# Mixture-of-experts stage: gather from x, one weight buffer more, other load and store shapes

## The chip, the cores and the metric

The kernel runs on one core of one Trainium2 chip. The metric is the device time of one execution in microseconds (us), the median of the runs that were made; lower is better. The profile comes from one further execution of the same program.

## The reference

The model is a float32 transformer over 256 tokens of 1024 channels: a first block of two layers, then a second block whose last part is a mixture of experts. Only that last part is touched. 32 experts stand in 4 groups of 8; every token is sent to the best two experts of its best group. The weights of one expert are two 1024x512 matrices (gate, up) and one 512x1024 matrix (down), 6 MB together, so all experts are 192 MB that must be read from HBM once.

```python
def rmsnorm_2(x, g):
    xf = x.astype(jnp.float32)
    y = xf * lax.rsqrt(jnp.mean(xf * xf, axis=-1, keepdims=True) + EPS)
    return (y * g.astype(jnp.float32)).astype(x.dtype)

def hier_moe(h, w_rg, b_rg, w_re, b_re, w_gate, w_up, w_down):
    ...
    weights = p_grp * top_p / jnp.sum(top_p, axis=-1, keepdims=True)
    expert = grp * EXPERTS_PER_GROUP + top_i
    ...
    def run_block(args):
        e, tok, w = args
        xb = xt[tok]
        hid = jax.nn.silu(xb @ w_gate[e]) * (xb @ w_up[e])
        return (hid @ w_down[e]) * w[:, None].astype(xb.dtype)
    ...

def second_block(...):
    ...
        x = x + hier_moe(rmsnorm_2(x, g_moe[l]), w_router_group[l], ...)
    return rmsnorm_2(x, g_final)
```

## The kernel before, in words

The kernel is one long program over the stages of the model; the stage `moe` is its last. The 32 experts are worked on in 8 groups of four (`for p in range(8)`). Each of the four gets 32 token slots, so that the 128 slots of a group fill the 128 columns of a TensorE operand.

**Routing.** `xT = self.xtile("h", "rT")` holds x transposed. It lives in the tile that the pool `xpool` hands out under the tag "xTh"; the pool has one buffer per tag, so a later tile of that tag takes the same memory once every reader of the earlier one is done. 16 matmuls called `rt` read it, eight for each half of the tokens. VectorE (DVE) makes from them the choice of experts (`A`), the place of each token in its expert's slots (`rk`) and the mixing weights (`Wt`).

**Gather.** `xk` is x times the reciprocal root mean square `r` of each token, with its channels reordered. It is written by two ScalarE (ACT) instructions (L1378) into the tile "xTh". `oh` is a one-hot matrix of tokens by slots (L1390), and the matmuls `xg` multiply `xk` by it; DVE copies the result, times the norm's gain, to `xe`, the gathered tokens (L1401).

**Weights.** They come in loads of 1 MB (one expert's half of a matrix, 128 partitions by 2048 numbers, 8 KB in one run for each partition). All are issued on one queue, that of SyncE (SP), and each is issued only after the one before it was issued (`self.after(*self.queue)`), in the order gate, up, down, group by group. A load goes to the next buffer of a rotation, `wrot`, through `wtile`, and its issue waits until the readers of that buffer's earlier contents are done. SP works through its queue in order: while one issue waits, those behind it wait as well. Before each issue SP also waits for the load eight issues earlier, since the semaphores DMAHW0 to DMAHW7 are used in turn. Three gate loads are issued earlier, by `moe_loads`. The rotation begins with

```python
self.wrot = (self.early + self.trot[:1] + [b, lambda: self.xtile("l", "w"), b, b]
             + hb + mw[4:5] + hb + [mw[i] for i in (8, 7, 0, 3, 2, 1, 5, 6)])
self.nw = 2
```

`self.early` has three entries, the buffers of the early loads, so the first load of the stage itself takes entry 3, counted from 0. There are 21 entries. `b` and `hb` are buffers that the stages before this one used for weights too, `xtile("l", ...)` is the tile "xTl".

**A group.** The matmuls `gu` multiply `xe` by gate and up; DVE and ACT make silu(gate) times up; it is transposed (`hT`); the matmuls `y` multiply it by down; two matmuls `acc` for each half of the channels scatter the result, weighted, to the tokens (`ot`, made from `oh` times `Wt` in `scatter`).

**The last group.** Its last 4 MB of up and its 8 MB of down are loaded in 256 KB pieces, runs of 2 KB (`pieces(..., True)`, L1425). Down is taken by halves of the output channels: when half `h` is done, x is added (`xo`, in tile "xTh", L1505), and `final` makes the final norm: squares on ACT (L1748), a root on ACT (L1754), four small steps on DVE, the products (L1532, L1535, L1536), and four stores of 256 KB (L1538).

Of the kernel before, what the change touches and what calls it, by code (L numbers as in the profile page):

```python
# [8 lines left out]
F32 = mybir.dt.float32  # L9
# [3 lines left out]
AF = mybir.ActivationFunctionType  # L13
OP = mybir.AluOpType
# [3 lines left out]
P = 128  # L18
S = 256
D = 1024  # L20
# [24 lines left out]
class K:  # L45
# [1270 lines left out]
    def moe(self, x):  # L1316
        nc, a = self.nc, self.a
        V = nc.vector
# [10 lines left out]
        def w1(i):  # L1329
# [4 lines left out]
        mw = [w1(i) for i in range(9)]  # L1334
        mp = self.pool("moe", 1, ctx)
        hb = [lambda: self.hbpool.tile([P, 2048], F32, tag="wh", name="w")] * 2
        self.wrot = (self.early + self.trot[:1] + [b, lambda: self.xtile("l", "w"), b, b]
                     + hb + mw[4:5] + hb + [mw[i] for i in (8, 7, 0, 3, 2, 1, 5, 6)])
        self.nw = 2

# [32 lines left out]
        acc = self.accs(pctx)  # L1373


        xk = self.xtile("h", "xk").rearrange("p (t k n) -> p t k n", t=2, k=8)
        for t in range(2):
            nc.scalar.activation(xk[:, t], x[:, t].rearrange("s (p k) -> s k p", k=8), AF.Copy, scale=r[:, t:t + 1])  # L1378
        oh = {}

        def four(m):
            return m.rearrange("p t (i n) -> p t i n", i=4)

        def over(m, p):
            return m[:, :, 4 * p:4 * p + 4, None].to_broadcast([P, 2, 4, CAP])

        def gather(p):

            oh[p] = mp.tile([P, 2, P], F32, tag=f"oh{p % 2}", name="oh")
            V.tensor_tensor(four(oh[p]), io[:, None, None].to_broadcast([P, 2, 4, CAP]), over(rk, p), op=OP.is_equal)  # L1390
            xe = mp.tile([P, 8, P], F32, tag="xe", name="xe")
            yield xe
            n = 4 if p else 2
            for c in range(2):
                for k0 in range(4 * c, 4 * c + 4, n):
                    ps = self.ps("xg")[:, 0:n * P].rearrange("p (k n) -> p k n", k=n)
                    for i in range(n):
                        for t in range(2):
                            self.mm(ps[:, i], xk[:, t, k0 + i], oh[p][:, t], t == 0, t == 1)
                    ks = slice(k0, k0 + n)  # L1400
                    V.tensor_tensor(xe[:, ks], ps, self.gcol8[:, ks, None].to_broadcast([P, n, P]), op=OP.mult)  # L1401
                yield

        def scatter(p):
# [7 lines left out]
            V.tensor_copy(ot, ps[:, 0:256].rearrange("p (t n) -> p t n", t=2))  # L1412
            return ot

        def pieces(src, fine):


            n1, n2 = src[0].shape[1:]
            if not fine:
                return [self.first.pop(0) if self.first else self.load(v) for v in src]  # L1420
            w = [self.wtile(n1, n2) for _ in src]
            for k in range(n1):
                for i in range(4):
                    with self.after(*self.queue):
                        self.queue = [nc.sync.dma_start(w[i][:, k], src[i][:, k]).ins]  # L1425
            return w

        def part(m, k, i):
            return m[:, k, CAP * i:CAP * i + CAP]
# [1 line left out]
        nxt = gather(0)  # L1431
        xe = next(nxt)
        next(nxt)
        Wt = next(routes)
        for p in range(8):
            last = p == 7
            y = self.gpool.tile([P, 2, 512], F32, tag="gain", name="y")
# [1 line left out]
            for w in (wg, wu):  # L1439
                ps = self.ps("gu")  # L1440
                for c in range(2):
                    ch = pieces([self.in_rows(w[4 * p + i], c) for i in range(4)], last and w is wu and c == 1)
                    for k in range(4):
                        for i in range(4):
                            self.mm(ps[CAP * i:CAP * i + CAP, :], part(xe, 4 * c + k, i), ch[i][:, k],
                                    c == 0 and k == 0, c == 1 and k == 3, tile_position=(0, CAP * i))
                    next(nxt, None)
                hs.append(ps)
# [1 line left out]
            s = y[:, 0]  # L1450
            nc.scalar.activation(s, hs[0], AF.Silu)  # L1451
            sk = y[:, 1].rearrange("s (k p) -> s k p", k=4)
            turn = "s (k p) -> s k p" if last else "s (p k) -> s k p"
            V.tensor_tensor(sk, s.rearrange(turn, k=4), hs[1].rearrange(turn, k=4), op=OP.mult)  # L1454
            ot = scatter(p)
            if not last:
                nxt = gather(p + 1)
                xe = next(nxt)
                next(nxt)
                next(nxt)  # L1460
            else:
                self.tc.keep_in_program_order(nc.scalar.preload_act_table_set("sqrt_and_others"))
                gf = self.final_gain()
                o = self.wtile(2, D)
                xo = self.xtile("h", "xo").rearrange("p (t n) -> p t n", t=2)
                fin = Norm(self, xo, None, None, (), pool=mp)
            ps = self.ps("hT")
            for f in range(4):
# [12 lines left out]
            def back(h):  # L1481
# [4 lines left out]
                for t in range(2):  # L1486
                    self.mm(acc[t][h], ot[:, t], y[:, h], p == 0, last)

            if not last:
                for c in range(2):  # L1490
                    ch = pieces([self.out_rows(wd[4 * p + i], c) for i in range(4)], False)
                    for k in range(2):
                        for h in range(2):
                            down(h, 2 * c + k, [v[:, :, h * 512:(h + 1) * 512] for v in ch], k)
                for h in range(2):
                    back(h)
            else:
                for h in range(2):
                    cs = slice(h * 512, (h + 1) * 512)
                    ch = pieces([wd[4 * p + i, :, cs].rearrange("(k p) n -> p k n", p=P) for i in range(4)], True)  # L1500
                    for k in range(4):
                        down(h, k, ch, k)
                    back(h)
                    for t in range(2):
                        V.tensor_tensor(xo[:, t, cs], x[:, t, cs], acc[t][h], op=OP.add)  # L1505
                        self.final(xo, gf, o, fin, t, h)
        pctx.close()
        self.spill(x, xo, nrm, r, rk, A, Wt, mp, gf, o)
        ctx.close()

    def final_gain(self):
# [9 lines left out]
            nc.scalar.activation(w[:, 0, cs], ps, AF.Copy)  # L1521
        return w[:, 0]

    def final(self, x, g, o, fin, t, c):

        nc = self.nc
        V = nc.vector
        xs, gs, os_ = [[v[:, t, k * 512:(k + 1) * 512] if v is not g else v[:, k * 512:(k + 1) * 512]
                        for k in range(2)] for v in (x, g, o)]
        fin.rms_part(t, c)  # L1530
        if c == 0:
            nc.gpsimd.tensor_tensor(os_[0], xs[0], gs[0], op=OP.mult)  # L1532
            return
        r = fin.r[:, t:t + 1]
        V.scalar_tensor_tensor(os_[1], xs[1], r, gs[1], op0=OP.mult, op1=OP.mult)  # L1535
        nc.scalar.activation(os_[0], os_[0], AF.Copy, scale=r)  # L1536
        for k in range(2):
            nc.sync.dma_start(self.out[0, t * P:(t + 1) * P, k * 512:(k + 1) * 512], os_[k])  # L1538

    def spill(self, x, xo, nrm, r, rk, A, Wt, mp, gf, o):  # L1540

# [12 lines left out]
        with tc.If(most > CAP):  # L1554
            with tc.tile_pool(name="spd", bufs=1, space=bass.MemoryType.DRAM) as dp:
# [47 lines left out]
                            V.scalar_tensor_tensor(xs, y, we[:, t], xs, op0=OP.mult, op1=OP.add)  # L1603
                fin = Norm(self, xo, None, None, (), pool=mp)
                for t in range(2):
                    for c in range(2):
                        self.final(xo, gf, o, fin, t, c)

    def lazy(self, f, *a):
        yield  # L1610
# [78 lines left out]
class Norm:  # L1689
# [49 lines left out]
    def rms_part(self, t, c):  # L1739
# [11 lines left out]
            V.tensor_scalar(ss, ss, EPS, None, op0=OP.add)  # L1751
            return

        nc.scalar.activation(u, y, AF.Sqrt, bias=ss)  # L1754
        V.tensor_scalar(v, y, ss, -0.5, op0=OP.add, op1=OP.mult)
        V.reciprocal(y, u)
        V.tensor_scalar(u, y, y, v, op0=OP.mult, op1=OP.mult)
# [400 lines left out]
```

## Time and profile before

| | |
|---|---|
| median of 3 runs | 1354.72 us (1354.0 to 1354.75) |
| the profiled execution's own time | 1352.86 us |
| its span (first to last event of the trace) | 1351.2 us |
| TensorE busy | 1238.8 us, 92% of the span |
| mean granted TensorE clock | 0.972 of full speed |
| loads from HBM | 343.38 MB |

The span is what the trace shows; 1.66 us of the profiled execution's time lie outside it. The median of the runs is 1.86 us above the profiled execution. A pair of figures such as 950.00:1300.00 is a stretch in us from the start of the span. The share of an engine is a mean over stages that differ: a stretch is read by its own rows.

### The profile page before, as it was taken

The page shows a single profiled execution, that of the slowest core. Times are in us where ns is not written, and L with a number is a line of the kernel's source. Part 1 is how long each engine was busy: PE and PEld are TensorE (multiplying, and loading weights), DVE is VectorE, ACT ScalarE, POOL GpSimd, SP SyncE. Part 2 cuts the span into 40 slices and gives each one's busy share as a digit, 9 for nine tenths or more (in the row PEclk, how much of TensorE's full clock was granted, in tenths as well). Part 3 has the DMA queues.
Part 4 walks back from the last instruction along what each step waited for, and adds up shares of the span by engine and source line. Part 5 has one row for each costly group of instructions (what it writes and reads, how often), then busy time and mean ns, then how long its engine had stood idle before and what let it go on. Part 6 is the DMA issues. An engine that isn't in the chain of part 4 may idle for free.

```text
span 1351.2 us, 20184 instructions
## 1 busy us (share of the span) xinstructions
PE 1238.8 (92%) x8427; PEld 917.3 (68%) x8427; DVE 647.6 (48%) x1137; ACT 485.3 (36%) x784; POOL 47.3 (4%) x72
## 2 busy tenths in 40 slices
PE   8899999999999999999999999999777778778886
PEld 7786899999998899999999998964122212222211
DVE  9955866666589766666776587431000001000001
ACT  3273644444577544444556565440000000000002
POOL 4010000000100000000300000000000000000000
PEclk9989999999999999999999999999999898999888
DMA  9401955544434765544562758789999999999996
GB/s 267 105 7 48 355 183 191 191 131 150 141 125 156 271 222 190 191 130 136 168 188 94 242 196 284 287 322 422 421 422 421 422 421 422 421 422 421 421 389 241
DMA packets 143436, 345.79 MB, mean 256 GB/s; under 512 B 9863, under 2 KB 100063, under 8 KB 120302
## 3 DMA queue, kind: packets, MB, share of 16 engines
q1 hardware_dynamic: 141418, 339.40, 68.2%
q0 software_dynamic: 1888, 5.06, 1.3%
q8 instruction: 67, 1.10, 0.3%
q14 instruction: 27, 0.22, 0.1%
q10 hardware_dynamic: 36, 0.01, 0.0%
HBM read 343.38 MB, written 1.06 MB: 255 GB/s over the span
## 4 chain that ended last, share of the span: by engine, by line
PE 62%; DMA 27%; DVE 7%; ACT 3%; issue 1%; SPq 0%; DVEq 0%; ACTq 0%
PE gu L77 21%; PE acc L77 15%; DMA w<-in_w_exp_down_dram 9%; DMA w<-in_w_exp_gate_dram 7%; DMA w<-in_w_exp_up_dram 7%; PE z L77 4%; PE qk L77 3%; PE y L77 3%; PE v L77 2%; PE mqk L77 2%; PE prj L77 2%; DMA b<-in_w_exp_gate_dram 1%; DMA b<-in_w_exp_up_dram 1%; PE psT L1711 1%; PE cq L77 1%
## 5 line engine op out<-in xcount | busy, mean ns | idle before, releaser
L182 DVE TENSOR_TENSOR wh<-w,wh 128x1024 fp32r<-128x1024 f32 x229 | 276.1, 1223 | 136.3 <-ACT wh L181 136.1
L181 ACT ACTIVATE wh<-w 128x1024 fp32r<-128x1024 f32 x229 | 236.7, 1055 | 194.4 <-PE gu L77 68.0
L77 PE MATMUL gu<-fxh,wh 128*128 128x256 f32 x1408 | 253.3, 281 | 0.7 <-ACT fxh L181 0.7
L77 PE MATMUL gu<-w,xe 128*32 128x512 f32 x920 | 178.6, 668 | 50.5 <-DMA w<-in_w_exp_gate_dram 28.0
L77 PEld LDWEIGHTS gu<-fxh,wh 128*128 128x128 f32 x1408 | 217.9, 190 | 1.7 <-ACT fxh L181 0.9
L77 PE MATMUL gu<-fxl,wh 128*128 128x256 f32 x704 | 197.8, 281 | 0.0
L77 PEld LDWEIGHTS gu<-w,xe 128*32 128x32 f32 x920 | 39.6, 120 | 168.1 <-issue 67.5
L77 PEld LDWEIGHTS gu<-fxl,wh 128*128 128x128 f32 x704 | 133.1, 189 | 0.8
L77 PE MATMUL y<-w,hT 128*32 128x512 f32 x456 | 103.1, 611 | 17.3 <-DMA w<-in_w_exp_down_dram 11.9
L77 PE MATMUL acc<-wh,hh 128*128 128x512 f32 x352 | 109.5, 393 | 0.0
L77 PEld LDWEIGHTS y<-w,hT 128*32 128x32 f32 x456 | 24.4, 110 | 88.5 <-DMA w<-in_w_exp_down_dram 42.1
L77 PEld LDWEIGHTS acc<-wh,hh 128*128 128x128 f32 x352 | 64.4, 188 | 12.3
L1412 DVE COPY ot<-owT 128x256 f32<-128x256 f32 x8 | 3.4, 425 | 138.4 <-PE owT L1410 138.4
L77 PE MATMUL acc<-wh,hl 128*128 128x512 f32 x176 | 68.6, 390 | 0.0
L1454 DVE TENSOR_TENSOR y<-y,gu 128x512 f32<-128x512 f32 x8 | 8.1, 1013 | 110.6 <-PE gu L77 100.8
L1451 ACT ACTIVATE y<-gu 128x512 f32<-128x512 f32 x8 | 4.8, 597 | 151.9 <-PE gu L77 151.9
L1485 DVE COPY y<-y 128x512 f32<-128x512 f32 x7 | 4.8, 692 | 105.9 <-PE y L77 105.9
L1471 ACT ACTIVATE hT<-hT 128x512 f32<-128x512 f32 x8 | 4.8, 597 | 137.5 <-PE hT L1469 137.5
L77 PE MATMUL qk<-oxh,wh 128*128 128x256 f32 x256 | 49.1, 287 | 0.0
L77 PE MATMUL z<-mxh,wh 128*128 128x256 f32 x256 | 47.7, 285 | 0.0
L1483 ACT ACTIVATE y<-y 128x512 f32<-128x512 f32 x9 | 5.4, 597 | 114.6 <-PE y L77 114.6
L77 PE MATMUL gu<-b,xe 128*32 128x512 f32 x104 | 37.8, 682 | 7.1 <-DMA b<-in_w_exp_gate_dram 4.2
(539 smaller groups left out, 2047.3 us busy)
## 6 DMA issues: line engine op xcount, KB each, us to landing
w<-in_w_exp_gate_dram SPq DMA_DIRECT2D x57, 1024.0 KB, 19.8
w<-in_w_exp_up_dram SPq DMA_DIRECT2D x54, 1024.0 KB, 19.8
w<-in_w_exp_down_dram SPq DMA_DIRECT2D x51, 1024.0 KB, 19.8
w<-in_ffn_w_gate_dram SPq DMA_DIRECT2D x22, 1024.0 KB, 5.7
w<-in_ffn_w_up_dram SPq DMA_DIRECT2D x22, 1024.0 KB, 6.8
w<-in_ffn_w_down_dram SPq DMA_DIRECT2D x22, 1024.0 KB, 5.1
w<-in_w_in_dram SPq DMA_DIRECT2D x20, 1024.0 KB, 5.9
w<-in_odd_w_in_dram SPq DMA_DIRECT2D x12, 1024.0 KB, 7.3
```

The lines of the kernel that those rows point to most:

```text
L77: self.lastmm = self.nc.tensor.matmul(out, lhsT, rhs, start=start, stop=stop, **kw).ins
L181: return (self.nc.scalar.activation(h, src, AF.Copy).ins, (eng or self.nc.vector).tensor_tensor(l, src, h.bitcast(F32), op=OP.subtract).ins)
L182: (eng or self.nc.vector).tensor_tensor(l, src, h.bitcast(F32), op=OP.subtract).ins)
L1412: V.tensor_copy(ot, ps[:, 0:256].rearrange("p (t n) -> p t n", t=2))
L1451: nc.scalar.activation(s, hs[0], AF.Silu)
L1454: V.tensor_tensor(sk, s.rearrange(turn, k=4), hs[1].rearrange(turn, k=4), op=OP.mult)
L1471: nc.scalar.activation(hT, ps.rearrange("p (f n) -> p f n", f=4), AF.Copy)
L1483: nc.scalar.activation(y[:, h], yps[h], AF.Copy)
L1485: V.tensor_copy(y[:, h], yps[h])
L1711: k.turned = k.nc.tensor.transpose(ps[:, i * P:(i + 1) * P], xg[:, t, (4 * c + i) * P:(4 * c + i + 1) * P], k.ident).ins
```

## The change

Five things change, all in the last stage.

1. The gather's matmuls read x itself (a reordered view). `oh` is multiplied by `r` instead (a new DVE instruction for each group), and the mixing weights are divided by `r` once (`ri`, `Wr`), so that `oh` times `Wr` is what it was. The two ACT instructions that wrote `xk` are gone. The second half of the routing is put behind an `xe` copy.
2. The tile "xTh" becomes a 22nd entry of `wrot`, between the third `b` and `hb`, that is entry 8.
3. The last group's up, and the first half of its down, come in 1 MB loads with runs of 8 KB, as in the other groups. The other 4 MB of down come in four loads of 1 MB, each over the four experts, in runs of 2 KB.
4. `xo` takes a buffer of the rotation.
5. The final norm is split in two functions: the second half does both token tiles' roots before the ACT products, and there is one store of 512 KB for each token tile.

```diff
-        self.wrot = (self.early + self.trot[:1] + [b, lambda: self.xtile("l", "w"), b, b]
+        self.wrot = (self.early + self.trot[:1] + [b, lambda: self.xtile("l", "w"), b, b, lambda: self.xtile("h", "w")]
                      + hb + mw[4:5] + hb + [mw[i] for i in (8, 7, 0, 3, 2, 1, 5, 6)])
...
-        xk = self.xtile("h", "xk").rearrange("p (t k n) -> p t k n", t=2, k=8)
-        for t in range(2):
-            nc.scalar.activation(xk[:, t], x[:, t].rearrange("s (p k) -> s k p", k=8), AF.Copy, scale=r[:, t:t + 1])
+        xk = x.rearrange("s t (p k) -> s t k p", k=8)
...
             V.tensor_tensor(four(oh[p]), io[:, None, None].to_broadcast([P, 2, 4, CAP]), over(rk, p), op=OP.is_equal)
+            self.lastoh = V.tensor_tensor(oh[p], oh[p], r[:, :, None].to_broadcast([P, 2, P]), op=OP.mult).ins
...
-        Wt = next(routes)
+
+        ri = mp.tile([P, 2], F32, name="ri")
+        with self.after(self.lastxe):
+            V.reciprocal(ri, r)
+            Wr = next(routes)
+        Wt = mp.tile([P, 2, 32], F32, name="Wr")
+        V.tensor_tensor(Wt, Wr, ri[:, :, None].to_broadcast([P, 2, 32]), op=OP.mult)
...
-                xo = self.xtile("h", "xo").rearrange("p (t n) -> p t n", t=2)
+                xo = self.wtile(2, D)
...
+            for c in range(1 if last else 2):
+                ch = pieces([self.out_rows(wd[4 * p + i], c) for i in range(4)])
+                for k in range(2):
+                    for h in range(2):
+                        down(h, 2 * c + k, [v[:, :, h * 512:(h + 1) * 512] for v in ch], k)
...
+            for h in range(2):
+                cs = slice(h * 512, (h + 1) * 512)
+                for k in range(2, 4):
+                    ch = self.load(wd[4 * p:4 * p + 4, :, cs].rearrange("i (p k) n -> k p i n", k=4)[k])
+                    down(h, k, [ch[:, i:i + 1] for i in range(4)], 0)
+                back(h)
+                for t in range(2):
+                    V.tensor_tensor(xo[:, t, cs], x[:, t, cs], acc[t][h], op=OP.add)
+                    if h == 0:
+                        self.final_first(xo, gf, o, fin, t)
+            self.final_second(xo, gf, o, fin)
...
+    def final_second(self, x, g, o, fin):
 
         nc = self.nc
         V = nc.vector
...
+        for t in range(2):
+            fin.rms_part(t, 1)
+            V.scalar_tensor_tensor(o[:, t, 512:], x[:, t, 512:], fin.r[:, t:t + 1], g[:, 512:], op0=OP.mult,
+                                   op1=OP.mult)
+        for t in range(2):
+            with self.after(fin.root):
+                nc.scalar.activation(o[:, t, 0:512], o[:, t, 0:512], AF.Copy, scale=fin.r[:, t:t + 1])
+            nc.sync.dma_start(self.out[0, t * P:(t + 1) * P, :], o[:, t])
```

**SP's queue at the first group's loads, before.** In brackets stand the semaphores that SP waits for ahead of an issue: PE_49 counts instructions of TensorE, Activation_49 of ACT, DVE_49 of DVE, DMAHW0_49 to DMAHW7_49 landed loads of this queue (the ending _49 says nothing). The first four rows are gate loads of the first group, the others its up loads and the first three of down.

```order
L95 DMA w<-in_w_exp_gate_dram 128x2048 [waits DMAHW5_49,DVE_49]
L95 DMA w<-in_w_exp_gate_dram 128x2048 [waits PE_49]
L95 DMA w<-in_w_exp_gate_dram 128x2048 [waits DMAHW0_49,DVE_49]
L95 DMA w<-in_w_exp_gate_dram 128x2048 [waits DMAHW6_49,DMAHW2_49,DVE_49]
L95 DMA w<-in_w_exp_up_dram 128x2048 [waits DMAHW7_49,PE_49]
L95 DMA w<-in_w_exp_up_dram 128x2048 [waits PE_49]
L95 DMA w<-in_w_exp_up_dram 128x2048 [waits DMASW4_49,DMASW5_49,DVE_49,DMAHW1_49,PE_49,Pool_49]
L95 DMA w<-in_w_exp_up_dram 128x2048 [waits PE_49,Activation_49]
L95 DMA w<-in_w_exp_up_dram 128x2048 [waits DMAHW3_49,DVE_49,PE_49]
L95 DMA w<-in_w_exp_up_dram 128x2048 [waits DVE_49,DMAHW4_49,PE_49,Activation_49]
L95 DMA w<-in_w_exp_up_dram 128x2048 [waits DMAHW5_49]
L95 DMA w<-in_w_exp_up_dram 128x2048 [waits DMAHW6_49,PE_49,Pool_49]
```

**The same place of the changed kernel**, from the same gate load on.

```order
L95 DMA w<-in_w_exp_gate_dram 128x2048 [waits DMAHW5_49,DVE_49]
L95 DMA w<-in_w_exp_gate_dram 128x2048 [waits PE_49]
L95 DMA w<-in_w_exp_gate_dram 128x2048 [waits DMAHW0_49,DVE_49]
L95 DMA w<-in_w_exp_gate_dram 128x2048 [waits DMAHW6_49,DMAHW2_49,DVE_49]
L95 DMA w<-in_w_exp_up_dram 128x2048 [waits DMAHW7_49,PE_49,Activation_49]
L95 DMA w<-in_w_exp_up_dram 128x2048
L95 DMA w<-in_w_exp_up_dram 128x2048 [waits DMAHW1_49]
L95 DMA w<-in_w_exp_up_dram 128x2048 [waits DMASW4_49,DMASW5_49,DVE_49,Pool_49]
L95 DMA w<-in_w_exp_up_dram 128x2048 [waits DMAHW3_49]
L95 DMA w<-in_w_exp_up_dram 128x2048 [waits DMAHW4_49,DVE_49]
L95 DMA w<-in_w_exp_up_dram 128x2048 [waits DMAHW5_49]
L95 DMA w<-in_w_exp_up_dram 128x2048 [waits DMAHW6_49]
```

The order of the loads stands as it was. The first up load has got a wait for ACT beside that for PE, and the up loads behind it, most of which waited for PE before, wait for it no more: a wait is left out where one ahead of it in the same queue covers it. In the built program the count of PE_49 that the first up load waits for is that of the last matmul `rt`, and the count of Activation_49 that of the last copy into `rT`.

**SP's queue at the end of the last group**, as a difference (- before, + changed). L1425 are the 256 KB loads, L1516 and L1517 the final norm's gain.

```order
-L1516 DMA w<-in_g_final_dram 1x1024
-L1425 DMA w<-in_w_exp_down_dram 128x512 x17
...
-L1538 DMA out_dram<-w 128x512 x4
...
+L1517 DMA w<-in_g_final_dram 1x1024
+L95 DMA w<-in_w_exp_down_dram 128x2048 x4
+L95 DMA w<-in_w_exp_down_dram 128x4x512 x4
...
+L1541 DMA out_dram<-w 128x1024 x2
```

The 32 pieces of down have become eight loads, the four stores two.

**DVE at the first gather, before**, from the slots `rk` on (the rows from L1303 to L1313 are the second half of the routing):

```order
L1371 SCALAR_TENSOR_TENSOR rk<-rk,A 128x64
L1390 TENSOR_TENSOR oh<-io,rk 128x256 x2
L1303 RECIPROCAL gs<-gs 128x2
...
L1313 TENSOR_TENSOR Wt<-Wt,o_9193 128x64
L1401 TENSOR_TENSOR xe<-xg,gcol_1347 128x256 x4
```

**and in the changed kernel:**

```order
L1371 SCALAR_TENSOR_TENSOR rk<-rk,A 128x64
L1389 TENSOR_TENSOR oh<-io,rk 128x256 x2
L1390 TENSOR_TENSOR oh<-oh,nr 128x256 x2
L1401 TENSOR_TENSOR xe<-xg,gcol_1347 128x256 x2
L1429 RECIPROCAL ri<-nr 128x2
```

Two products by `r` (here `nr`) have come in front of the first `xe` copies, and the routing's second half has moved behind them.

## Rows read from the trace of the kernel before

**Rows 1.** The page: GB/s in 40 slices, chain by engine.

```profile
GB/s 267 105 7 48 355 183 191 191 131 150 141 125 156 271 222 190 191 130 136 168 188 94 242 196 284 287 322 422 421 422 421 422 421 422 421 422 421 421 389 241
...
PE 62%; DMA 27%; DVE 7%; ACT 3%; issue 1%; SPq 0%; DVEq 0%; ACTq 0%
```

**Rows 2.** Windows: stretch, length, busy by engine, then PEclk, DMA share, GB/s.

```profile
905.00:1301.00 396.00, 316.95 (x1709) 100.53 (x1709) 29.79 (x52) 13.11 (x22) 0.00 (x0) 0.94 1.01 421
1301.00:1337.00 36.00, 33.06 (x136) 8.25 (x134) 2.81 (x8) 5.14 (x10) 2.55 (x2) 0.95 0.99 358
```

**Rows 3.** The chain in order of time: start us, us, what.

```profile
964.60 19.80 DMA w<-in_w_exp_gate_dram
```

**Rows 4.** SP's waits from 800 on: us in total, times, longest.

```profile
SPq L95 <- PE gu L77: 22.7, 16, 13.9
```

**Rows 5.** Timeline of SP's queue, issues merged: start us, us, what.

```profile
842.01 10.07 SPq L95 DMA_DIRECT2D w<-in_w_exp_gate_dram  x4
860.03 20.70 SPq L95 DMA_DIRECT2D w<-in_w_exp_up_dram  x8
881.05 23.43 SPq L95 DMA_DIRECT2D w<-in_w_exp_down_dram  x7
```

**Rows 6.** Timeline of SP's queue, the one issue from 903 to 904.

```profile
903.67 0.33 SPq L95 DMA_DIRECT2D w<-in_w_exp_down_dram  x1
```

**Rows 7.** Windows of 1 us around that issue, columns as in rows 2.

```profile
899.00:900.00 1.00, 0.00 (x0) 0.00 (x0) 0.97 (x6) 0.56 (x1) 0.00 (x0) 1.00 0.24 98
...
904.00:905.00 1.00, 1.00 (x11) 1.00 (x10) 0.21 (x1) 0.00 (x0) 0.00 (x0) 1.00 0.66 115
905.00:906.00 1.00, 1.00 (x10) 0.61 (x13) 0.53 (x2) 0.00 (x0) 0.00 (x0) 1.00 0.75 213
906.00:907.00 1.00, 1.00 (x16) 0.38 (x12) 0.44 (x2) 0.00 (x0) 0.00 (x0) 1.00 0.91 377
907.00:908.00 1.00, 1.00 (x16) 0.27 (x11) 0.00 (x0) 0.00 (x0) 0.00 (x0) 1.00 1.05 442
```

**Rows 8.** ACT's timeline at the copy xk, and the matmuls that read tile rT.

```profile
891.96 4.21 ACT L1378 ACTIVATE xk<-x,nr 128x1024 f32<-128x1024 f32 x2 [1.05 <-PE rt L77]
...
L77 PE MATMUL rt<-wr,rT x32: 194/279/300, 887.8 to 891.6; 128*128 128x36 f32 x32
```

**Rows 9.** Windows with 2 KB runs (first two) and 1 KB runs; one issue.

```profile
774.00:775.00 1.00, 1.00 (x11) 1.00 (x10) 0.00 (x0) 0.93 (x1) 0.00 (x0) 1.00 1.06 371
775.00:776.00 1.00, 1.00 (x11) 1.00 (x10) 0.84 (x1) 0.13 (x1) 0.00 (x0) 1.00 1.05 365
141.00:142.00 1.00, 1.00 (x7) 0.82 (x6) 1.00 (x2) 1.00 (x3) 0.00 (x0) 1.00 1.11 350
...
773.17 0.38 SPq L95 DMA_DIRECT2D w<-in_w_proj_gla_dram  x1
```

**Rows 10.** Weight loads of TensorE at half and full clock; a window of 2 us.

```profile
1295.21 0.20 PEld L77 LDWEIGHTS gu<-w,xe 128*32 128x32 f32 x4 [0.66 <-issue]
...
1304.76 0.13 PEld L77 LDWEIGHTS gu<-w,xe 128*32 128x32 f32 x4 [0.30 <-issue]
...
1292.00:1294.00 2.00, 1.34 (x2) 0.00 (x0) 0.00 (x0) 0.00 (x0) 0.00 (x0) 0.58 1.01 422
```

**Rows 11.** The tail: last matmuls y, last acc in the chain, the stores.

```profile
1337.78 1.04 PE L77 MATMUL y<-w,hT 128*32 128x512 f32 x2
...
1339.51 1.14 PE acc L77 x2
...
1344.03 2.71 SPq L1538 DMA_DIRECT2D out_dram<-w  x4
```

**Rows 12.** Timeline at the first gather: one-hot, first gu, oh times weights.

```profile
895.76 0.76 DVE L1390 TENSOR_TENSOR oh<-io,rk 128x256 f32<-128x256 f32 x2
...
900.02 0.62 PE L77 MATMUL gu<-w,xe 128*32 128x512 f32 x2 [1.55 <-DVE xe L1401]
...
906.02 0.42 DVE L1407 TENSOR_TENSOR oh<-oh,Wt 128x256 f32<-128x256 f32 x1
```

More of the change, by code (lines that the diff above doesn't have):

```diff
@@ L1400, in gather @@
                     ks = slice(k0, k0 + n)
-                    V.tensor_tensor(xe[:, ks], ps, self.gcol8[:, ks, None].to_broadcast([P, n, P]), op=OP.mult)
+                    self.lastxe = V.tensor_tensor(xe[:, ks], ps, self.gcol8[:, ks, None].to_broadcast([P, n, P]),
+                                                  op=OP.mult).ins
                 yield
@@ L1413, in scatter, with pieces @@
             return ot
[L1415 to L1426, printed above, removed]
+        def pieces(src):
+            return [self.first.pop(0) if self.first else self.load(v) for v in src]
         def part(m, k, i):
@@ L1441, in moe @@
                 for c in range(2):
-                    ch = pieces([self.in_rows(w[4 * p + i], c) for i in range(4)], last and w is wu and c == 1)
+                    ch = pieces([self.in_rows(w[4 * p + i], c) for i in range(4)])
                     for k in range(4):
@@ L1452, in moe @@
             sk = y[:, 1].rearrange("s (k p) -> s k p", k=4)
-            turn = "s (k p) -> s k p" if last else "s (p k) -> s k p"
+            turn = "s (p k) -> s k p"
             V.tensor_tensor(sk, s.rearrange(turn, k=4), hs[1].rearrange(turn, k=4), op=OP.mult)
@@ L1487, in back @@
                     self.mm(acc[t][h], ot[:, t], y[:, h], p == 0, last)
-            if not last:
[L1490 to L1494, printed above, removed]
+            for c in range(1 if last else 2):
[3 more added lines that the diff above has]
+                        down(h, 2 * c + k, [v[:, :, h * 512:(h + 1) * 512] for v in ch], k)
+            if not last:
                 for h in range(2):
                     back(h)
[L1497 to L1506, printed above, removed]
+                continue
+            for h in range(2):
[9 more added lines that the diff above has]
+            self.final_second(xo, gf, o, fin)
         pctx.close()
-        self.spill(x, xo, nrm, r, rk, A, Wt, mp, gf, o)
+        self.spill(x, xo, nrm, r, rk, A, Wr, mp, gf, o)
         ctx.close()
@@ L1522, in final_gain, with final_first @@
         return w[:, 0]
-    def final(self, x, g, o, fin, t, c):
+    def final_first(self, x, g, o, fin, t):
+        fin.rms_part(t, 0)
+        self.nc.gpsimd.tensor_tensor(o[:, t, 0:512], x[:, t, 0:512], g[:, 0:512], op=OP.mult)
+    def final_second(self, x, g, o, fin):
         nc = self.nc
         V = nc.vector
[L1528 to L1538, printed above, removed]
+        for t in range(2):
[6 more added lines that the diff above has]
+            nc.sync.dma_start(self.out[0, t * P:(t + 1) * P, :], o[:, t])
     def spill(self, x, xo, nrm, r, rk, A, Wt, mp, gf, o):
@@ L1605, in spill @@
                 for t in range(2):
-                    for c in range(2):
-                        self.final(xo, gf, o, fin, t, c)
+                    self.final_first(xo, gf, o, fin, t)
+                self.final_second(xo, gf, o, fin)
     def lazy(self, f, *a):
@@ L1752, in rms_part @@
             return
-        nc.scalar.activation(u, y, AF.Sqrt, bias=ss)
+        self.root = nc.scalar.activation(u, y, AF.Sqrt, bias=ss).ins
         V.tensor_scalar(v, y, ss, -0.5, op0=OP.add, op1=OP.mult)
```

## The prediction, made blind

> **What bounds the kernel now.** I read the page first, for where the last stage stands: of 40 slices the last 13 or so move 420 GB/s, and the chain gives 27% of the span to DMA [rows 1]. The windows then say how steady that is: from 905 to 1301 us the DMA engines are busy all the time and move 421 GB/s; from 1301 to 1337, where the 256 KB pieces run, 358 GB/s, also with a DMA share of 0.99 [rows 2]. So from 905 on the time is bytes by rate, and TensorE, busy 317 of 396 us, follows. The chain shows how the queue is kept full: a link of 19.8 us for each load [rows 3], the time from issue to landing with eight loads in flight (SP waits for the load eight issues earlier), so 19.88 us, issue to issue, for eight: 2.485 us for 1 MB. Last, SP's own rows: waits for TensorE to free a buffer are 22.7 us over 16 waits [rows 4], and one is most of them. Seven down loads stand in a row of issues that spans 23.43 us from 881.05 [rows 5]; the sixth of the first group's down is issued only at 903.67 [rows 6], when the first gate buffers are free. By the windows behind it, 115, 213, 377 and 442 GB/s in four us are 1147 kB, 2.7 us at 421, so the stream runs again, in effect, from 908.0 - 2.7 = 905.3, 1.6 us after the issue [rows 7].
>
> What the reader has to take along: every us by which the stream of loads is late at 905 is a us at the end, since nothing behind it has slack.
>
> **The 22nd buffer.** The stage's first load takes entry 3 of the rotation, so entry 8 is for its sixth load. Five loads go ahead: one gate load, then the four of the row at 842.01; the sixth is the first up load, issued at 860.03 in the profile [rows 5]. Entry 8 is now the tile "xTh", and until the router is through it holds `rT`. The load may not start before the last `rt` has read it. The trace shows that wait in the kernel before as well, on another engine: `xk` went into the same tile, and ACT sat idle until `rt` was done and started it at 891.96; the `rt` matmuls run from 887.8 to 891.8 (the last starts at 891.6) [rows 8]. The rows of the changed queue say the same: the first up load has got ACT and PE to wait for, and the loads behind it need no PE wait of their own, since this one covers theirs.
>
> SP works in order. So behind this one load stand all others: seven up and the down loads, which in the profile were issued from 860.03 on and had landed when the stream ran dry near 899 [rows 7]. Count them: eight up, and five of the seven down of the row at 881.05, as the sixth is the issue of 903.67 [rows 5, 6]: 13 loads.
>
> Step by step: the first up load is issued at 891.9 instead of 860.0. With 1.6 us to the stream in effect [rows 7], 893.5. 13 loads at 2.485 are 32.3 us, so the fourteenth, which in the profile begins at 905.3, begins at 925.8. **Term 1: +20.5 us.** No hole is left for it to make up: with a 22nd buffer six down loads find a free one, and the next needs the first gate buffers, free at about 903 [rows 6], long before its turn (it is the fifteenth; its issue also waits for the landing of the seventh, about 893.5 + 7 x 2.485 = 911). TensorE waits for up instead, which costs nothing of its own: a group of 24 loads lasts 59.6 us in the stream, and TensorE is busy 317 us of 396 there with its waits for halves of a weight counted in [rows 2]. Bounds: if the wait ended with the first half of `rt`, near 889.6 (in the middle of its 887.8 to 891.6), 2.3 less; if the restart of eight queued loads were slower than that of 903.67, perhaps 1 more. So +18.2 to +21.5. From DMA's side, the idle stretch grows from 6 us (98 of 421 GB/s in the us from 899 put its start at 899.2 [rows 7]) to over 30, as the gate loads issued by 852 [rows 5] land long before 893.5.
>
> **The gather from x.** Two ACT instructions of 4.21 us together go [rows 8]; two DVE products come in, 0.42 us each by the product of the same size, behind the one-hots (895.76 to 896.52) [rows 12]. The first `gu` starts at 900.02 now [rows 12], held by `xe`, which DVE made behind the routing's second half; this half now comes later. One product (896.94), about two us of `xg` and a copy of 0.42 give 899.4, some 0.6 earlier. As the stream decides, this is worth nothing, cover and all: without the wait for "xTh" it would be 0.6 of the hole. The products in the later groups lie on DVE, which is busy 30 us of 396 [rows 2]: nothing.
>
> **The last group's runs.** The 12 MB of 256 KB pieces take, in the profile, from about 905.3 + 159 x 2.485 = 1300.4 (171 loads of 1 MB less 12 are left at 905.3) to about 1336.4, 36.0 us, or 350 GB/s with the thinning end, in which the last pieces land one by one. Of these, 8 MB go over to 8 KB runs: 8 x 2.485 = 19.9 us. The other 4 MB keep runs of 2 KB but come in loads of 1 MB. For that shape the trace has a row: `w_proj_gla` and its neighbour, the same shape, move 365 to 371 GB/s with the engines full, and 1 KB runs of 1 MB loads 350 [rows 9]: 4.19 MB at 368 are 11.4 us, with 0.6 for the thinning end 12.0. Together 31.9. **Term 2: -4.1 us.** Bounds: -3.5 (the 4 MB at the pieces' 350, the end included), -5.5 (at 421).
>
> Here a page of the Trainium skill speaks against the change. DMA: Bandwidth & Descriptors, section Specifications, gives 512 B as the smallest transfer at line rate. By it 2 KB and 8 KB runs would be alike, and term 2 would be 0. The rows at 350, 368 and 421 GB/s, each with full engines, disagree, so I give it a rival's chance only.
>
> **The tail.** `xo` in the rotation costs no wait: its buffer's readers are the last group's gate matmuls or earlier. The stores: of four issues in 2.71 us [rows 11] two go, and the last comes about 0.4 us sooner; the roots are taken together, but DVE's products stand between the two tokens' small steps as before. I take -0.3. The last load now brings four matmuls in place of one, side by side in four column strips, about as long as the 1.04 us of the last one [rows 11]. Against that stands the clock. With 1 MB loads TensorE idles between landings; in the profile's stretch of 1 MB loads the granted clock fell to 0.58 (half clock, 1.2 GHz, most of the time) while single matmuls waited for landings [rows 10], whereas it was 1.0 through most of the small pieces. At half clock weight loads follow at 0.86 us instead of 0.43 (duration plus idle) [rows 10], so the last `y` would cost some 0.6 more and the last `acc`, 1.14 us [rows 11], 1.1 more. Half of these 1.7 is 0.8. **Term 3: +0.5 us**, bounds -0.5 and +2.
>
> **Sum.** 20.5 - 4.1 + 0.5 = +16.9 us on the profiled execution's 1352.86, 1369.8; the median of the runs is 1.86 above it, so I expect 1354.72 + 16.9 = 1371.6. The bounds together: 18.2 - 5.5 - 0.5 = +12.2 and 21.5 - 3.5 + 2.0 = +20.0.
>
> **The rivals.**
>
> *The loads are not held (faster).* If the first up load left near 860 as it does now, the 22nd buffer would do what it is for: one more down load, 2.5 us, ahead of the hole, and the first buffers free 0.6 us sooner, so that 3.1 of its 6 us go; with terms 2 and 3, 3.1 + 4.1 - 0.5 = -6.7, 1348.0. It decides if that load is issued before about 871: from there on each later us is one lost. For it speaks the hole, which is real [rows 6, 7]; against it ACT's idle time ahead of `xk`, in the same tile [rows 8].
>
> *Runs of 8 KB bring nothing.* The stream would go on at the pieces' rate, because something in the last group and not the run's length sets it: +20.5 + 0.5 = +21.0, 1375.7. For it: the DMA engines are as busy there, 0.99, as before [rows 2]. Against it the rows of 1 KB and 2 KB runs, at other places of the program, with the same order of rates [rows 9]. This is what the page's 512 B would make of it.
>
> *The lost time is partly given back.* TensorE, not the stream, might set the pace between 905 and 945, where it frees buffers just in time; then a later stream would lose less than 20.5. But the windows have the stream at 421 from 905 on [rows 2], so nothing is there to give back; at most the 2.3 us of term 1's bound. This lies in the range.
>
> **How the numbers follow.** Held, with the terms as above: 0.90. Runs without effect: 0.05. Not held: 0.04. Terms that happen to cancel: 0.01. A measurement of this kernel tells 0.2%, 2.7 us, from no change; so slower 0.95, same 0.01, faster 0.04. The range for 8 in 10 reaches from 1366, just under the low bounds (1354.72 + 12.2 = 1366.9), to 1376, the second rival; the high bounds, 1374.7, lie inside.
>
> **What would show it.** In the changed kernel's profile SP's queue should have no weight load issued between 852 and 891, then eight in a row; the DMA row should be near 0 from some 860 to 893; then 421 GB/s without a gap to some 1341, a last 4 MB at about 368, a last landing near 1353. TensorE should idle before `gu` on up loads at about 909. ACT should show no 4.2 us copy. Wrong I would be if the first up load stood near 860, if DMA still had its 6 us hole near 900, or if the stream showed room (a rate below 421) behind it.

## The result, and the profile after

The changed kernel takes 1370.47 us in the median of four runs (1369.33 to 1372.10), the kernel before beside it 1354.36 (1352.20 to 1354.75): a ratio of 1.0126, with a 95% interval of 1.0113 to 1.0139, so slower by 15 to 19 us. Its profiled execution took 1372.10 us, with a span of 1370.4.

In these two executions the program ahead of the stage, which is the same code, ran 1.57 us later in the changed kernel (its four gate loads begin at 843.58, before at 842.01 [rows 5]). Wherever times of two executions are compared below, that shift of the first gate loads is taken out and called the offset.

The page, GB/s in 40 slices and the chain by engine, which answers to [rows 1]:

```profile
GB/s 266 100 7 48 353 190 194 192 131 123 139 124 154 295 243 185 187 122 120 170 185 124 205 252 269 44 369 422 420 421 422 422 421 421 422 421 421 421 421 248
...
PE 55%; DMA 34%; DVE 7%; ACT 3%; issue 1%; SPq 0%; DVEq 0%; ACTq 0%
```

The 26th slice, 287 GB/s before, is at 44: the stream starts later, and the chain gives DMA more of the span, 34% for 27%.

SP's queue in the timeline, issues merged (start us, us, what), which answers to [rows 5, 6]:

```profile
843.58 10.07 SPq L95 DMA_DIRECT2D w<-in_w_exp_gate_dram  x4
893.50 4.27 SPq L95 DMA_DIRECT2D w<-in_w_exp_up_dram  x8
898.45 18.68 SPq L95 DMA_DIRECT2D w<-in_w_exp_down_dram  x8
```

Four gate loads, then nothing for 40 us, then eight up loads in a row. Before, the first of them left at 860.03. What the queue waited for stands in SP's waits from 800 on (us in total, times, longest) and in the rows of the tile rT, which answer to [rows 4, 8]:

```profile
SPq L95 <- PE rt L77: 39.8, 1, 39.8
L77 PE MATMUL rt<-wr,rT x32: 194/279/300, 889.3 to 893.2; 128*128 128x36 f32 x32
```

The last `rt` starts at 893.2, and 0.3 us later the first up load leaves.

Windows of the same kernel (stretch, length, busy by engine, clock, DMA share, GB/s), which answer to [rows 2, 7]:

```profile
858.00:893.00 35.00, 35.00 (x250) 32.52 (x248) 12.70 (x27) 17.14 (x43) 0.46 (x5) 1.00 0.06 25
893.00:894.00 1.00, 1.00 (x10) 1.00 (x10) 0.65 (x4) 0.78 (x1) 0.00 (x0) 1.00 0.00 0
894.00:895.00 1.00, 1.00 (x11) 1.00 (x10) 0.97 (x8) 0.00 (x0) 0.00 (x0) 1.00 0.68 115
895.00:896.00 1.00, 0.30 (x3) 0.12 (x2) 0.93 (x5) 0.00 (x0) 0.00 (x0) 1.00 0.82 287
896.00:897.00 1.00, 0.17 (x3) 0.17 (x3) 0.68 (x4) 0.00 (x0) 0.00 (x0) 1.00 0.97 410
896.00:1341.00 445.00, 367.36 (x1842) 141.80 (x1842) 38.34 (x82) 16.48 (x29) 0.00 (x0) 0.95 1.01 421
1343.00:1353.00 10.00, 8.35 (x50) 2.10 (x50) 0.32 (x2) 0.29 (x2) 0.00 (x0) 1.00 1.04 389
1353.00:1354.00 1.00, 0.35 (x1) 0.30 (x2) 0.00 (x0) 0.59 (x1) 0.00 (x0) 1.00 0.67 254
1354.00:1355.00 1.00, 1.00 (x3) 0.38 (x2) 0.19 (x1) 0.00 (x0) 0.00 (x0) 1.00 0.56 215
1355.00:1356.00 1.00, 1.00 (x6) 0.16 (x8) 0.83 (x2) 0.47 (x1) 0.36 (x1) 1.00 0.41 158
1356.00:1357.00 1.00, 0.62 (x8) 0.00 (x0) 0.44 (x2) 0.81 (x4) 1.00 (x2) 1.00 0.04 16
```

For 35 us the DMA engines are all but idle, 25 GB/s. The three us from 894 move 812 kB, 1.9 us at 421 GB/s, so the stream runs in effect from 897.0 - 1.9 = 895.1, 1.6 us after the issue. From there to 1341 it is 421 GB/s without a gap. The last 4 MB, runs of 2 KB in loads of 1 MB, move at 389, until the stream thins out: the four us from 1353 move 643 kB.

TensorE's timeline at the first gather, which answers to [rows 12]:

```profile
898.58 4.04 PE L77 MATMUL xg<-oh,x 128*128 128x128 f32 x16 [0.33 <-DVE oh L1390]
902.55 0.62 PE L77 MATMUL gu<-w,xe 128*32 128x512 f32 x2
```

Less the offset, the first `gu` starts at 900.98. Before it was 900.02.

And the tail, which answers to [rows 11]:

```profile
1357.07 1.06 PE L77 MATMUL y<-w,hT 128*32 128x512 f32 x8 [0.45 <-DMA w<-in_w_exp_down_dram]
...
1358.85 1.98 PE L77 MATMUL acc<-y,ot 128*128 128x512 f32 x4 [0.72 <-ACT y L1481]
...
1363.46 1.98 SPq L1541 DMA_DIRECT2D out_dram<-w  x2
```

The last `y` starts 19.29 us later than at 1337.78, 17.7 without the offset. From there to the end it is 13.33 us, before 13.42 (1351.2 - 1337.78).

### The profile page after: what moved, and what is told of

It is laid out like the page before. It is cut to its first block, busy times and chain, and to the rows that moved or that the text cites. A ratio compares the mean times of both kernels' runs of the same rounds, so it can differ in the third digit from the quotient of the medians.

```text
span 1370.4 us, 20136 instructions
## 1 busy us (share of the span) xinstructions
PE 1262.4 (92%) x8427; PEld 949.8 (69%) x8427; DVE 651.9 (48%) x1147; ACT 481.3 (35%) x782; POOL 47.4 (3%) x72
## 3 DMA queue, kind: packets, MB, share of 16 engines
HBM read 343.38 MB, written 1.06 MB: 251 GB/s over the span
## 4 chain that ended last, share of the span: by engine, by line
PE 55%; DMA 34%; DVE 7%; ACT 3%; issue 1%; SPq 0%; DVEq 0%; ACTq 0%
PE gu L77 18%; PE acc L77 14%; DMA w<-in_w_exp_gate_dram 10%; DMA w<-in_w_exp_up_dram 10%; DMA w<-in_w_exp_down_dram 10%; PE z L77 4%; PE qk L77 2%; PE v L77 2%; PE mqk L77 2%; PE prj L77 2%; DMA b<-in_w_exp_up_dram 1%; DMA b<-in_w_exp_down_dram 1%; DVE wh L182 1%; PE psT L1714 1%; PE cq L77 1%
## 5 line engine op out<-in xcount | busy, mean ns | idle before, releaser
L77 PE MATMUL gu<-w,xe 128*32 128x512 f32 x944 | 169.8, 657 | 45.7 <-DMA w<-in_w_exp_gate_dram 37.3
L77 PE MATMUL y<-w,hT 128*32 128x512 f32 x448 | 100.2, 615 | 17.9 <-DMA w<-in_w_exp_down_dram 13.1
L77 PEld LDWEIGHTS xg<-oh,x 128*128 128x128 f32 x256 | 62.2, 334 | 8.0 <-issue 7.5
L77 PE MATMUL xg<-oh,x 128*128 128x128 f32 x256 | 64.7, 405 | 0.3 <-DVE oh L1390 0.3
```

The source lines that it names most:

```text
L77: self.lastmm = self.nc.tensor.matmul(out, lhsT, rhs, start=start, stop=stop, **kw).ins
```

## The experiments

The theory: the whole loss is the first up load, which waits for the router's last read of "xTh" with 12 other loads behind it. The main rival: the loss comes from other parts of the change, the slower `xg` or the last group. All times below are beside the kernel before on the same chip. A ratio is not that of the two medians, and a difference in us that is worked out from it can differ from theirs by up to 1 us.

**1. The entry taken out again (no_h).**

```diff
-        self.wrot = (self.early + self.trot[:1] + [b, lambda: self.xtile("l", "w"), b, b, lambda: self.xtile("h", "w")]
+        self.wrot = (self.early + self.trot[:1] + [b, lambda: self.xtile("l", "w"), b, b]
```

> The changed kernel without the 22nd entry: 21 weight buffers as before, everything else as changed. Theory (the first up load held for the router costs the 20 us): the up loads leave near 860 again, the 6 us hole near 900 is back and about 1 us longer, since the gather's matmuls now take 4.04 us where they took 1.95; the last group's loads save 2.8; so 1352.5 us, ratio 0.9985 (0.997 to 1.000). Rival (the loss comes from the slower gather or from the last group's new loads and stores): it stays near 1370, ratio 1.012.

Measured: 1349.80 us against 1354.33, ratio 0.9968 (0.9956 to 0.9980). The loss is gone, and all that is left of the change makes a gain. SP's queue:

```profile
860.46 20.69 SPq L95 DMA_DIRECT2D w<-in_w_exp_up_dram  x8
...
906.26 0.80 SPq L95 DMA_DIRECT2D w<-in_w_exp_down_dram  x2
```

The up loads leave as before. The first gate buffer is free late, at 906.26, 2.2 us later than 903.67 without the offset of 0.43: 1.0 for the slower `xg`, and the rest because in this execution the granted clock was 0.56 from 900 to 903, where it was 1.00 before. Two executions of one kernel, h_last and h_last_2 below, show that price: with clocks of 0.51 and 1.00 there, the first gate buffer is free at 905.83 and 904.63 without the offsets, 1.2 us apart. The gain is larger than forecast: the interval leaves out the 0.9985. By the trace it is smaller, 0.9 us (a span of 1350.7 against 1351.2, and the offset), but this profiled execution, at 1352.46, is the slowest of the six.

**2. The entry five places later (h_mid).**

```diff
-        self.wrot = (self.early + self.trot[:1] + [b, lambda: self.xtile("l", "w"), b, b, lambda: self.xtile("h", "w")]
-                     + hb + mw[4:5] + hb + [mw[i] for i in (8, 7, 0, 3, 2, 1, 5, 6)])
+        self.wrot = (self.early + self.trot[:1] + [b, lambda: self.xtile("l", "w"), b, b]
+                     + hb + mw[4:5] + hb + [lambda: self.xtile("h", "w")] + [mw[i] for i in (8, 7, 0, 3, 2, 1, 5, 6)])
```

> The same 22 buffers with the tile xTh five entries later (entry 13, first filled by the sixth up load). Theory (the delay is the number of loads behind the wait times 2.485): eight loads stand behind the wait in place of 13, so 20.5 - 5 x 2.485 = 8.1 us lost, 2.8 of it won back in the last group: 1359.7 us, ratio 1.004 (1.002 to 1.006). Rival (the loss is a fixed price of the wait, whatever stands behind it): near 1370, ratio 1.012.

Measured: 1358.61, ratio 1.0032 (1.0021 to 1.0043), so +4.3 us. The interval takes in the forecast of 1.004 and leaves out the rival. The wait is the same, and so is its end: the queue issues three up loads from 892.25 on, where the changed kernel issues eight from 893.50.

```profile
892.25 1.28 SPq L95 DMA_DIRECT2D w<-in_w_exp_up_dram  x3
893.62 12.13 SPq L95 DMA_DIRECT2D w<-in_w_exp_down_dram  x8
```

Only what stands behind the wait has changed, eight loads in place of 13. From the changed kernel's 1.0126 that takes off 0.0094, 12.7 us (11.8 by the medians), against the 12.4 of five loads.

**3. The entry at the end of the rotation (h_last, and once more as h_last_2).**

```diff
-        self.wrot = (self.early + self.trot[:1] + [b, lambda: self.xtile("l", "w"), b, b, lambda: self.xtile("h", "w")]
-                     + hb + mw[4:5] + hb + [mw[i] for i in (8, 7, 0, 3, 2, 1, 5, 6)])
+        self.wrot = (self.early + self.trot[:1] + [b, lambda: self.xtile("l", "w"), b, b]
+                     + hb + mw[4:5] + hb + [mw[i] for i in (8, 7, 0, 3, 2, 1, 5, 6)]
+                     + [lambda: self.xtile("h", "w")])
```

> The same 22 buffers, but the tile xTh is the last entry of the rotation and not entry 8, so that it is first filled by the stage's 19th load, the sixth of down. Theory: only that load waits for the router; it leaves at about 892 where without the buffer it would leave near 904.5, so one load more fills the hole, 2.5 us less than with 21 buffers: 1350.0 us, ratio 0.9965 (0.995 to 0.9985). Rival (a 22nd buffer in this tile costs time wherever it stands): 1370 or at least no gain over 21 buffers, 1352.5.

> xTh as the last of 22 entries, once more, beside the two above: as in its first runs 1349.5, ratio 0.9961 (0.9948 to 0.9975). Whether its trace has the stretch at half clock again is open.

Measured: 1349.74, ratio 0.9961 (0.9948 to 0.9975), and 1348.51, 0.9967 (0.9955 to 0.9979). So the tile costs nothing where only late loads wait for it. SP's queue in the second of these runs (h_last_2), the sixth and the seventh down load:

```profile
891.90 0.33 SPq L95 DMA_DIRECT2D w<-in_w_exp_down_dram  x1
...
904.59 0.33 SPq L95 DMA_DIRECT2D w<-in_w_exp_down_dram  x1
```

The buffer does here what it is for: the sixth load leaves when the router is through, and only the seventh waits for the first gate buffer. But the 2.5 us that this should bring over 21 buffers can't be seen in the times (0.9961 and 0.9967 against 0.9968), whose intervals are that wide. By the traces of no_h and h_last, both with the clock at half near 900, the last `y` starts 2.4 us earlier (1334.66 against 1337.35, with 0.30 of offset).

**4. The last group's loads alone (loads_only).** The kernel before, with the last half of up and the first half of down in loads of 1 MB and 8 KB runs, and the second half of down so:

```diff
-                    ch = pieces([wd[4 * p + i, :, cs].rearrange("(k p) n -> p k n", p=P) for i in range(4)], True)
-                    for k in range(4):
-                        down(h, k, ch, k)
...
+                for k in range(2, 4):
+                    ch = self.load(wd[4 * p:4 * p + 4, :, cs].rearrange("i (p k) n -> k p i n", k=4)[k])
+                    down(h, k, [ch[:, i:i + 1] for i in range(4)], 0)
...
```

> The kernel before with the changed last group's load shapes alone (1 MB loads in 8 KB runs, four loads of 1 MB in 2 KB runs); gather, buffers, xo and stores as before. Prediction's term 2: -4.1 us, 1350.3. Theory after the result: -2.8, 1351.6, ratio 0.998. Rival (8 KB runs bring nothing): 0, ratio 1.000.

Measured: 1349.71, ratio 0.9965 (0.9952 to 0.9979), so -4.7 us (-2.8 to -6.5). The rival, no effect, is out. The traces put the gain lower. SP's timeline, the issue that ends the hole:

```profile
902.91 0.81 SPq L95 DMA_DIRECT2D w<-in_w_exp_down_dram  x2
```

and TensorE's, the last `y`:

```profile
1334.34 1.04 PE L77 MATMUL y<-w,hT 128*32 128x512 f32 x8
```

From the issue that ends the hole to the last `y` it is 431.4 us; before it was 1337.78 - 903.67 = 434.1 [rows 6, 11], in stores_only (below, with the old loads) 434.4, and in no_h (new loads) 431.1. That is -2.7 to -3.3. Counted to the last `acc`, two more runs with the old loads (gather_only and gather_contig, below) can be set beside these. TensorE's rows of loads_only and of gather_only:

```profile
1336.10 1.98 PE L77 MATMUL acc<-y,ot 128*128 128x512 f32 x4 [0.72 <-ACT y L1483]
...
1341.41 1.98 PE L77 MATMUL acc<-y,ot 128*128 128x512 f32 x4 [0.69 <-ACT y L1490]
```

From the issue that ends the hole it is 432.87 us in no_h and 433.19 in loads_only, and with the old loads 435.84 before, 436.11 in stores_only, 436.24 in gather_contig and 436.83 in gather_only: -2.7 to -4.0 us.

This run changes the length of the runs and the size of the loads together. Windows of the kernel before, for its 256 KB pieces without the end of the stream:

```profile
1301.00:1334.00 33.00, 30.06 (x127) 7.70 (x126) 2.81 (x8) 5.14 (x10) 2.55 (x2) 0.95 1.01 367
```

Runs of 2 KB move 367 GB/s in these pieces and 365 to 389 in loads of 1 MB ([rows 9] and the changed kernel's end), against 421 for runs of 8 KB. That speaks for the length of the run, but no experiment changes it alone.

**5. The held load alone (h_old_tail).** The changed kernel with the last group's loads, the final norm and the stores of before (their part of the diff undone):

```diff
-                for k in range(2, 4):
-                    ch = self.load(wd[4 * p:4 * p + 4, :, cs].rearrange("i (p k) n -> k p i n", k=4)[k])
-                    down(h, k, [ch[:, i:i + 1] for i in range(4)], 0)
+                    ch = pieces([wd[4 * p + i, :, cs].rearrange("(k p) n -> p k n", p=P) for i in range(4)], True)
+                    for k in range(4):
+                        down(h, k, ch, k)
...
```

> The changed gather and the changed buffers (22, xTh at entry 8), with the last group's loads, the final norm and the stores as before. Theory (term 1 is the whole loss): +20.5 us and nothing won back, 1374.9 us, ratio 1.0151 (1.0135 to 1.0165). Rival (part of the changed kernel's +16.1 comes from its last group, and the held load costs less): 1370 or less, ratio 1.0115 or less. Its trace also shows once more how long the 256 KB pieces take (36.0 us in the trace of before).

Measured: 1373.72 against 1353.74, ratio 1.0144 (1.0129 to 1.0160), so +19.5 us (+17.5 to +21.7); the rival's 1.0115 lies outside. Its span, 1371.9, is 20.7 longer than before, 20.4 without the offset of 0.31. The gather and the `xo` of the change are in this run too, and experiment 6, which has them without the held load, finds no loss clear of the noise: term 1 is all of the loss.

**6. The gather alone (gather_only), and with neighbouring channels (gather_contig).** The kernel before with the gather from x, and `xo` in a buffer of the rotation, 21 buffers; the second differs from the first in this line:

```diff
-        xk = x.rearrange("s t (p k) -> s t k p", k=8)
+        xk = x.rearrange("s t (k p) -> s t k p", k=8)
```

> The kernel before with the gather from x alone (oh times r, Wr, routing's second half behind xe); 21 buffers, last group, final norm and stores as before. Prediction's step: first gu 0.6 us earlier, so 0.6 of the hole, 1353.8. Theory after the result: xg takes 4.04 in place of 1.95 us, first gu 1.0 later, the first gate buffers free 1.0 later and the hole 1.0 longer: 1355.4, ratio 1.0007; if the granted clock falls to half at the first gu, as in the trace with 21 buffers and the changed gather, 2.6 later: 1357.0, ratio 1.002.

> The same, but xg reads 128 neighbouring channels of x for each weight load in place of every eighth, so the channels are gathered in another order (the output is not that of the reference). Theory (reading every eighth number is what costs): the first 16 records of xg take 1.95 us again, as from xk. Rival (reading from the tile of x, or the order of work around it, costs): 4 us as with every eighth number.

Measured: gather_only 1354.67 against 1353.74, ratio 1.0008 (0.9999 to 1.0017), which can't be told from no change; gather_contig one run, 1350.67. The traces tell them apart. All matmuls `xg` by operation (ns: least, median, most), of gather_only:

```profile
L77 PEld LDWEIGHTS xg<-oh,x x256: 312/335/336, 896.9 to 1247.7; 128*128 128x128 f32 x128
L77 PE MATMUL xg<-oh,x x256: 397/402/504, 897.0 to 1247.8; 128*128 128x128 f32 x128
```

The same rows of gather_contig:

```profile
L77 PEld LDWEIGHTS xg<-oh,x x256: 186/192/192, 895.5 to 1242.5; 128*128 128x128 f32 x128
L77 PE MATMUL xg<-oh,x x256: 275/275/377, 895.6 to 1242.7; 128*128 128x128 f32 x128
```

Every eighth number of x as weights: 335 ns for a weight load. Neighbouring numbers of the same tile: 192. Nothing else differs, so the stride is what costs. On the path stands the issue that ends the hole, in SP's timeline of gather_only:

```profile
904.58 0.33 SPq L95 DMA_DIRECT2D w<-in_w_exp_down_dram  x1
```

and of gather_contig, with the gate loads that give its offset:

```profile
840.59 10.07 SPq L95 DMA_DIRECT2D w<-in_w_exp_gate_dram  x4
...
901.17 0.80 SPq L95 DMA_DIRECT2D w<-in_w_exp_down_dram  x2
```

Without the offsets (-0.05 and -1.42) these are 904.63 and 902.59, against 903.67 before: 1.0 us later with the stride, 1.1 earlier without.

**7. The final norm and the stores alone (stores_only).** The kernel before with `final_first` and `final_second`, as in the change:

```diff
-                        self.final(xo, gf, o, fin, t, h)
+                        if h == 0:
+                            self.final_first(xo, gf, o, fin, t)
+            if last:
+                self.final_second(xo, gf, o, fin)
```

> The kernel before with the two-part final norm and one store of 512 KB for each token tile alone. Prediction (term 3 without the clock): -0.3 us, 1354.1, ratio 0.9998. By the traces of the four runs so far the stretch from the last y to the end is 13.35 us with the new stores and 13.86 with the old ones behind the same loads: -0.5, ratio 0.9996. Rival (two larger stores end later, since neither can leave before its whole token tile is done): +0.5, ratio 1.0004. None of these can be told apart by the times; the tail's rows are to tell.

Measured: 1353.16 against 1353.74, ratio 0.9997 (0.9988 to 1.0006): no difference that can be measured. The last `y` starts at 1336.91 and the span is 1350.1, so 13.19 us in place of 13.42, -0.2.

**8. A quicker first gather behind the entry at the end (h_last_warm, h_last_xc).** First six more matmuls of ones ahead of the gather, then also a contiguous copy for the first half of the first gather:

```diff
-            self.warm(warm, 8)
+            self.warm(warm, 13)
...
-            self.warm(warm, 5)
+            self.warm(warm, 6)
...
+        xc = self.gpool.tile([P, 2, 512], F32, tag="gain", name="xc").rearrange("s t (k p) -> s t k p", k=4)
+        with self.after(nrm.root):
+            for t in range(2):
+                nc.scalar.activation(xc[:, t], xk[:, t, 0:4], AF.Copy)
...
+                            v = xc if p == 0 and c == 0 else xk
...
```

> xTh as the last of 22 entries, and six more matmuls of ones ahead of the first gather (13 and 6 in the two places that had 8 and 5), so that TensorE idles less between the router and the gather. In the trace of xTh as last entry the granted clock was 0.5 from 900 to 903 and the first gu, at 1.07 us a pair in place of 0.62, freed the first gate buffer at 905.96. Theory (that stretch at half clock costs the hole 1.2 us): clock 1.0 there, first gate buffer free at about 904.7, 1.2 us less than with xTh as last entry alone: about 1348.3, ratio 0.9955. Rival (the added matmuls push rk or xg back, or the clock falls as before): no gain, 1349.5, ratio 0.9963.

> As the one before, and for the first half of the first gather alone xg reads a contiguous copy of x, which ACT makes behind the second root (two copies of about 1 us); all other gathers read x itself. Theory: those eight matmuls (16 records) take 2.0 us in place of 4.04, so the first gu and the first free gate buffer come 2.0 us earlier and the hole is as much shorter: 2 us less than the one before, about 1346.3, ratio 0.994. Rival (the copies come too late for xg, or the next wait ends as late): no gain over the one before.

Measured: h_last_warm 1349.36 against 1353.58, ratio 0.9965 (0.9952 to 0.9979), no gain over h_last. Its clock was 1.00 at the first `gu`, but so it was in h_last_2 without the added matmuls: the fall in h_last's trace belongs to some executions and not to the code, and what sets it stays open.

h_last_xc 1347.29, ratio 0.9952 (0.9939 to 0.9966), 6.5 us less than before and the fastest here. Its first gather, in TensorE's timeline:

```profile
896.22 2.02 PE L77 MATMUL xg<-oh,xc 128*128 128x128 f32 x16
```

and the seventh down load, in SP's:

```profile
901.82 0.80 SPq L95 DMA_DIRECT2D w<-in_w_exp_down_dram  x2
```

The 4.04 us are 2.02, and the seventh load leaves at 902.61 without the offset of -0.79, 2.0 us before the 904.63 of h_last_2 (904.59, offset -0.04). The medians differ by 2.1 from h_last_warm, as forecast, but the intervals overlap, and in the profiled executions of h_last_xc and h_last_2 only 0.8 us are left at the last `y`; the size of this last step is not settled.

## Why the prediction was right, and where not

**Term 1, the held load.** As predicted, in place and in size. No weight load is issued up to the last `rt`, the stream runs 1.6 us behind the first issue, and there is no room behind it: 421 GB/s to 1341. h_old_tail gives +19.5 by the times and +20.4 by the trace for the predicted +20.5, and h_mid takes off 12.7 us for five loads less behind the wait. That it is the place in the queue, and not the tile, h_last shows: the same tile 13 loads later costs nothing.

**Term 2, the last group's runs.** -4.1 predicted, -4.7 measured with an interval of -2.8 to -6.5, -2.7 to -4.0 by the traces. The sign holds, and so do the rates, 421 GB/s for runs of 8 KB against 367 for the pieces; the size can't be told closer. Two sizes inside the term were off. I allowed 0.6 us for the thinning end; the 643 kB from 1353 on would take 1.7 us at 389 GB/s and take nearly four, so that it costs about 2. The rate of the 2 KB runs was taken at 368 and measured at 389, which gives back 0.6. The bound of -3.5 was worked out wrong, too: 4.19 MB at 350 GB/s, the end included, are 12.0 us, which is -4.1 again, and the traces lie partly outside it. The Trainium skill's 512 B for line rate (DMA: Bandwidth & Descriptors, Specifications) does not agree with these rows: 2 KB runs at 389 and 8 KB runs at 421 GB/s, both with the DMA engines full.

**Term 3, the tail.** +0.5 predicted, -0.2 by stores_only's rows. The step that failed is the clock: I gave half clock in the tail a half chance, and the granted clock stayed at 1.00 from 1343 past the last `acc`, the last `y` at 1.06 us for eight matmul records. The stores bring that -0.2, where I took -0.3.

**The gather from x.** This step was wrong, and the result hid it. I let `xg` take "about two us" and put the first `gu` 0.6 us earlier; it came 1.0 later, since every eighth number of x as weights takes 335 ns in place of 192. gather_contig shows the step's other half right: with neighbouring numbers `gu` does come earlier, by 1.1 us at the buffer. In the changed kernel it costs nothing, as the stream is held for longer than that; in gather_only, where the first gate buffers end the hole, it is 1.0 us at that issue, too little to be told in the times.

**The sum.** +20.4, -2.7 to -4.7, and -0.2 make +15.5 to +17.5; the medians give +16.1 and the ratio +17.1, the prediction +16.9.

**The rivals.** "Not held" is out by SP's row of 893.50. "Runs of 8 KB bring nothing" is out: the new loads gain 4.7 us in loads_only, and the rate does rise from 367 to 421 GB/s. "Partly given back" left no trace: 421 GB/s all through.

## What to carry to other kernels

A buffer that joins a rotation belongs where its earlier tenant is gone before its turn comes. One load that waits in an in-order queue costs what would have landed meanwhile, not what it brings itself. Here that was 13 loads of 2.485 us, 32.3 us, less the 11.8 us from 893.5 to 905.3 that the fourteenth had to wait anyway: 20.5. So read who holds the memory, and until when, before placing a load there: the same tile at the other end of the list took all of the 20 us away. A step whose cost lies under another's shadow should still be measured by itself, as the next change may take the shadow away.

## What the runs showed of the hardware

For TensorE, weights read from SBUF with a stride of eight numbers load in 335 ns for 128x128 float32, and in 192 ns from neighbouring numbers of the same tile; the 16 records of half a group's gather go from 2.02 to 4.04 us. And the granted clock at one and the same place of the same kernel can be 0.5 in one execution and 1.0 in the next (h_last and h_last_2, from 900 to 903: 0.51 and 1.00), so a row there is not read as the kernel's own from a single profile.
